# Writing the last third of a hybrid mixer in strict engine order, with its adaLN products placed one at a time

## The chip, the core and the metric

The kernel runs on one NeuronCore of a Trainium2 chip. The core has five engines, each with an instruction queue of its own: TensorE (PE; its weight loads are listed apart as PEld), VectorE (DVE), ScalarE (ACT), GpSimd (POOL) and SyncE (SP), which here issues nearly all DMA transfers. The metric is device time in microseconds (us) of one execution, lower is better; given is the median of several runs. A profiled execution has a span, from its first to its last instruction, and a time of its own.

## The reference

One decoder layer on 256 tokens (T) with 1024 channels (D), in float32. Nine vectors of 1024 come from `c @ w_ada + b_ada`: a shift, a scale and a gate for each of three parts.

```
h = rmsnorm(x, ffn1_norm) * (1 + sc1) + sh1
x = x + 0.5 * (1 + g1) * ((silu(h @ wg1) * (h @ wu1)) @ wd1)          # FFN 1, width 2816 = 22 * 128
h = rmsnorm(x, mix_norm) * (1 + sc2) + sh2
q_a, k_a, v_a, x_m, z = split(h @ w_in)                                # 5 times 512 columns
o_a = rmsnorm(attention(q_a, k_a, v_a), attn_norm)                     # 8 heads, causal
x_c = silu(causal_conv4(x_m))
h_m = groupnorm(mlstm(x_c, x_m)) * mlstm_norm                          # 4 heads
o_m = (h_m + mlstm_skip * x_c) * silu(z)
x = x + (1 + g2) * (concat(o_a, o_m) @ w_out)
h = rmsnorm(x, ffn2_norm) * (1 + sc3) + sh3
x = x + 0.5 * (1 + g3) * ((silu(h @ wg3) * (h @ wu3)) @ wd3)           # FFN 2
out = rmsnorm(x, final_norm)
```

With 256 tokens and blocks of 256, MoBA attention is plain causal attention. The mLSTM is computed for all 256 tokens at once instead of chunk by chunk.

## The kernel before

Everything is held transposed: channels on the 128 partitions, tokens along the free dimension, so x is 8 tiles of 128x256. Each product of a weight tile (128x128) with a tile of activations is done in three matmuls (`mm3`): weight and activation are each split in a high part in float32r and a low rest, and the matmuls are high x high, low x high, high x low.

**Weights.** They arrive as a fixed list of chunks of up to 128x2048 (1 MB), on the SP queue, into 4 buffers (`raw`). `weights()` takes the next chunk n: it issues the load of chunk n+3 and the split of chunk n+1, and returns chunk n. A split is done in pieces of 1024 columns: ScalarE copies the piece to float32r (`whi`), VectorE subtracts to get the rest (`wlo`). There are 5 buffers of each, so a piece can be split once the piece five before it has been used.

**adaLN products.** A vector element is 1024 products summed, so 128 of them are one VectorE instruction on a 128x1024 tile of w_ada (`ada`, 512 KB, 3 buffers), which writes 128 sums (output `junk` is not used). There are 72 of these. 16 (shift 1, scale 1) are written out at the start of FFN 1 and the last 8 (gate 3) belong to FFN 2; the 48 between stand in a list (`jobs`), and `side(0, 0)` takes the next two: their loads on SP and their products on VectorE. In order: gate 1, scale 2, shift 2, gate 2, scale 3, shift 3, eight each; behind the last of eight a small instruction or two finish the vector (`scale_fin`: tiles `fin`, `gs`; `shift_fin`: `sh`).

**Order.** A scheduler orders each engine's instructions at compile time, by its own estimate of the times. An engine wrapped in `Ordered` with `on` set pins each instruction behind the one written directly before it on the same engine (`keep_in_program_order`); instructions without a pin move wherever their data and buffers let them. DMA issues are always pinned. Inside the mixer the `ada` products are pinned too (`pinned`), each behind the VectorE instruction written just before it.

**The mixer's last third** stands at the end of `mixer`: value tile 1 (`values(1)`, generator `g0`), attention heads (`scores`, `turn` for the transposed probabilities, `weigh` for the product with the values, all by pairs of heads j), mLSTM heads (`m_scores`, `m_sums`, `m_vars`), then `a_out` (norm of the attention output: `rstd_of`, `oa`, split into `mix0` and `mix3`), four tiles of z (`tiles(shifted(zs...))`, each 24 `mm3` products' worth of matmuls in a "b" bank of PSUM, of which there are 2; `done` empties it with a `col` copy and a bias on ScalarE and a product `ht` on VectorE), `m_factors` (the norm factors of the mLSTM heads, a chain between ScalarE and VectorE on 4x256 tiles, which ends in `rows`), `z_silu`, and the product with w_out over four chunks c of two input tiles k each. Tiles k = 0 to 3 are `mix0` and `mix3`; k = 4, 5 come from `m_out(0)` and 6, 7 from `m_out(1)`, which multiply `cn` by the factors that `m_spread` puts in PSUM behind k = 1, add, multiply by silu(z) and split (`hh`, `hl`). Last, `residual` adds each output tile to x and forms the next FFN's input (`pre_h`: `hh`, `hl`) and its squares.

Before the change, TensorE, ScalarE and VectorE are pinned from `weigh(3)` to the first `next(g)` behind `a_out`, ScalarE and VectorE again in `m_factors` to `z_silu` and in the two `m_out`, and TensorE stays pinned up to c = 1. The splits of w_out and w_z, `m_sums(3)`, `m_skip`, the emptying of the z tiles and the residual are not.

Of the kernel before, what the change touches and what calls it, by code (L numbers as in the profile page):

```python
# [14 lines left out]
ALU = mybir.AluOpType  # L15
# [3 lines left out]
T = 256  # L19
# [42 lines left out]
def layer(ctx: ExitStack, tc: tile.TileContext, i, out: bass.AP):  # L62
    nc = tc.nc
    act, dve, pool, pe = (Ordered(tc, e) for e in (nc.scalar, nc.vector, nc.gpsimd, nc.tensor))
# [40 lines left out]
    x_sb = const([P, ND, T], F32, "x")  # L105
# [138 lines left out]
    gt = [const([P, ND], F32, f"gt{k}") for k in range(3)]  # L244
# [113 lines left out]
            eng.tensor_tensor(acc, acc, s, ALU.add)  # L358
        return s

    def residual(d, ps, g, k):
        dve.scalar_tensor_tensor(x_sb[:, d], ps, g[:, d:d + 1], x_sb[:, d], ALU.mult, ALU.add)
        if k is None:
            s = add_sq(d, pool)
            pool.tensor_scalar(fin_u[0][:, d], x_sb[:, d], sm[:, C_NF + d:C_NF + d + 1], None, ALU.mult)
            return s
        if k == 1:

            s = add_sq(d, pool)
            for j in range(2 * d - 6, 2 * d - 4) if 3 <= d < 6 else range(d, d + 1) if d >= 6 else ():  # L370
                pre_h(k, j)
        elif d == ND - 1:
            s = add_sq(d, pool)
            pre_h(k, d)
        else:
            pre_h(k, d)
            s = add_sq(d, pool)
        return s
# [26 lines left out]
    def ffn(k, nxt):  # L405
        nfa = 3
        with tc.tile_pool(name=f"g{k}", bufs=1) as gp:
            g2 = gp.tile([P, NF, 2, T], F32R, name=f"g2{k}")
            gh, gl = g2[:, :, 0], g2[:, :, 1]
            if k == 0:  # L410
# [34 lines left out]
                def keep(ft):  # L445
                    if ft % 2:
                        act.activation(half[:, ft], ps[ft], AF.Copy)
                    else:
                        dve.tensor_copy(half[:, ft], ps[ft])

                ps = [bank(t) for t in ring]
                r1 = rstd_of([sq[:, d] for d in (0, 1, 4, 5)], pre=False,
                             mid=lambda: (warm(16), ada(8), ada(0), load_to(0), scale_fin(0, 0, 1, pool),
                                         shift_fin(0, 0, 1, pool)))
# [21 lines left out]
                ps = [bank(t) for t in ring]  # L476
# [5 lines left out]
                        inner(w, f2, ps[2 * j + f2], 0, False)  # L482
                for d in range(4, 8):
                    w = weights()
                    side(1)
                    outer(w, ps, d, d == 7)

                late = [lambda ft=ft: finish(gh, gl, 8 + ft, ps[ft][:, 0:T], ps[ft][:, T:2 * T])
# [1 line left out]
                for j in range(4):  # L490
                    if j < 2:
                        late.pop(0)()
                        late.pop(0)()
                    w = weights()
                    if j == 3:
                        side(1)
                    for f2 in range(2):
                        ft = 2 * j + f2
                        pb = bank("a")
                        inner(w, f2, pb, 4, True)  # L500
                        o = half[:, ft]
                        dve.tensor_tensor(o, o, pb, ALU.add)
                        finish(gh, gl, ft, o[:, 0:T], o[:, T:2 * T])
                nfa = 16
            else:
                ps = [bank(t) for t in ("b", "b", "a", "a", "a", "a")]
# [56 lines left out]
    nxt_sq = [None]  # L563
# [3 lines left out]
    def side(*on):  # L567

        for o in on:
            if jobs:  # L570
                jobs.pop(0)(o)
# [9 lines left out]
    for c in range(2):  # L581
        w = weights()
        side(*[0] * (3 - 3 * c))
        for d4 in range(4):
            d = c * 4 + d4
# [10 lines left out]
    with tc.tile_pool(name="fin", bufs=1) as fp:  # L596
# [4 lines left out]
        r2 = r.unsqueeze(1).to_broadcast([P, 2, T])  # L601
# [5 lines left out]
def mixer(tc, nc, i, mp, L):  # L607
    act, dve, pool, pe, sp = L["act"], L["dve"], L["pool"], L["pe"], L["sp"]
# [3 lines left out]
    residual, newton, rstd_of, tables = L["residual"], L["newton"], L["rstd_of"], L["tables"]  # L612
    ident, ident_b, maskq, maskt, ohc, ohr = (L[k] for k in ("ident", "ident_b", "maskq", "maskt", "ohc", "ohr"))
    nxt_sq, r, px, acc2 = L["nxt_sq"], L["r"], L["px"], L["acc"]
    side, jobs = L["side"], L["jobs"]
# [1 line left out]
    def mt(shape, name, dt=F32, tag=None, bufs=1):  # L617
        return mp.tile(shape, dt, name=nm(name), tag=tag or name, bufs=bufs)

    def tiles(*done):  # L620

        w = weights()
        for g in range(2):
            pb = bank("b")
            for d in range(8):
                mm3(pb[:, 0:W], w, (g * 8 + d) * P, hh[:, d], hl[:, d], start=(d == 0), stop=(d == 7))
            done[g](pb)
            yield

    def shifted(dst):  # L630

        def done(pb):
            col = tmp.tile([P, 1], F32, tag="col", name=nm("col"), bufs=3)
            act.activation(col, pb[:, T:T + 1], AF.Copy)
            t = t256("ht", bufs=3)
            dve.tensor_tensor(t, r, pb[:, 0:T], ALU.mult)
            act.activation(dst, t, AF.Identity, bias=col)
        return done

    ones_h = mt([P, P], "ones_h")  # L640
# [83 lines left out]
    st = {}  # L724
# [68 lines left out]
    def m_sums(h):  # L793
        if h == 0:
            st["prow"] = bank("a")
        prow = st["prow"]
        pn = bank("b" if h == 3 else "m")
        pe.matmul(pn[:, 0:T], vm[:, 0, h], wE[h][:, 0:T], start=True, stop=False, skip_group_check=True)
        pe.matmul(pn[:, P:T], vm[:, 1, h], wE[h][:, T:384], start=False, stop=True, skip_group_check=True)
        pe.matmul(prow[0:4, 0:T], ohc[:, h], wE[h][:, 0:T], start=(h == 0), stop=False, skip_group_check=True)  # L800
        pe.matmul(prow[0:4, P:T], ohc[:, h], wE[h][:, T:384], start=False, stop=(h == NH - 1),
                  skip_group_check=True)
        act.activation(cn[:, h], pn[:, 0:T], AF.Copy, scale=sm[:, C_MN + h:C_MN + h + 1])
        s = st["sq", h] = t256("sq", bufs=3)
        act.activation(s, pn[:, 0:T], AF.Square)

    def m_vars(h):
        pe.matmul(st["prow"][0:4, T:2 * T], ohc[:, h], st["sq", h], start=False, stop=(h == NH - 1),
                  skip_group_check=True)

    def m_factors():


        prow, em = st["prow"], st["em"]
        act.on = dve.on = True
        dd = mt([NH, T], "dd", tag="R2")
        act.activation(dd, prow[0:4, 0:T], AF.Square, scale=EPS ** 0.5)
        dve.tensor_tensor(dd, dd, em, ALU.max)
        vv = mt([NH, T], "vv", tag="R3")
        dve.scalar_tensor_tensor(vv, prow[0:4, T:2 * T], 1.0 / P, dd, ALU.mult, ALU.add)  # L820
        rs = mt([NH, T], "rs", tag="R1")
        act.activation(rs, vv, AF.Ln)
        act.activation(rs, rs, AF.Exp, scale=-0.5)
        newton(rs, vv, [NH, T], "r", 0.0)
        spread(rs)
# [7 lines left out]
    zs = mt([P, NH, T], "zs")  # L833
# [15 lines left out]
    def m_out(h2):  # L849

        h = slice(2 * h2, 2 * h2 + 2)
        c = cn[:, h]
        dve.tensor_tensor(c, c, st["pb"][h2].rearrange("p (h t) -> p h t", t=T), ALU.mult)
        dve.tensor_tensor(c, c, xc[:, h], ALU.add)
        dve.tensor_tensor(c, c, zs[:, h], ALU.mult)
        k = slice(4 + 2 * h2, 6 + 2 * h2)
        hilo(hh[:, k, 0:T], hl[:, k, 0:T], c)
# [50 lines left out]
    def turn(j):  # L908

        for e in range(2):  # L910
            pt = bank("a")
            for b in range(3):
                pe.transpose(pt[:, b * P:(b + 1) * P], st["pr", j][:, e, b * P:(b + 1) * P], ident)
            pT = st["pT", j, e] = mt([P, 384], "pT", tag=f"pT{e}", bufs=2)
            act.activation(pT, pt[:, 0:384], AF.Copy)
# [15 lines left out]
            pool.tensor_tensor(acc2, acc2, s, ALU.add)  # L931

    def a_out():
        r2 = rstd_of([acc2, st["osq"]], ones_h, "a", pre=False)
        for j in range(4):
            o = oa[:, j, 0:T]
            dve.scalar_tensor_tensor(o, o, sm[:, C_AN + j:C_AN + j + 1], r2, ALU.mult, ALU.mult)

        mix3[:] = [mt([P, 3, T], name, F32R, tag="pr", bufs=2) for name in ("mix3h", "mix3l")]
        hilo(*mix0, oa[:, 0, 0:T])  # L940
        hilo(*mix3, oa[:, 1:4, 0:T])
# [3 lines left out]
    g = queries(0)  # L945
# [6 lines left out]
    g = queries(1)  # L952
# [11 lines left out]
    g = queries(2)  # L964
# [8 lines left out]
    g = queries(3)  # L973
# [17 lines left out]
    turn(2)  # L991
    m_scores(3)
    m_sums(1)
    g = tiles(shifted(zs[:, 0]), shifted(zs[:, 1]))
    side(0, 0, 0, 0, 0, 0)
    next(g)
    next(g0)
    turn(3)
    weigh(2)
    for e in (pe, act, dve):  # L1000
        e.on = True
    weigh(3)
    m_sums(2)
    m_vars(0)
    a_out()
    next(g)
    act.on = dve.on = False
    m_sums(3)
    m_skip()
    m_vars(1)  # L1010
# [6 lines left out]
    next(g)  # L1017
    z_silu(0)
    z_silu(1)
    act.on = dve.on = False  # L1020
    po = [bank(t) for t in ("m", "m", "a", "a")]
    for c in range(4):
        w = weights()
        side(*[0] * (0, 1, 2, 3)[c])
        pe.on = c < 2
        for k2 in range(2):
            k = c * 2 + k2
            for d in range(8):
                mm3(po[d // 2][:, (d % 2) * T:(d % 2 + 1) * T], w, (k2 * 8 + d) * P, *mix(k),
                    start=(c == 0 and k2 == 0 and d % 2 == 0), stop=(c == 3 and k2 == 1))  # L1030
                if (k, d) == (1, 7):
                    m_spread()
                    act.on = dve.on = True
                    m_out(0)
                    m_out(1)
                    act.on = dve.on = False
    side(*[0] * len(jobs))
    act.on = dve.on = True
    L["pre_shift"](2)
    act.on = dve.on = False  # L1040
    for d in range(8):
        nxt_sq[0] = residual(d, po[d // 2][:, (d % 2) * T:(d % 2 + 1) * T], L["gt"][1], 2)


# [84 lines left out]
```

## Time and profile before

| | |
|---|---|
| time, median of 3 runs | 532.76 us (532.58 to 534.71) |
| the profiled execution: time | 531.47 us |
| the profiled execution: span | 529.7 us |
| granted TensorE clock, mean | 0.995 |
| busy: PE, DVE, ACT, POOL | 97%, 80%, 53%, 9% |

The span is some 1.8 us shorter than the execution's own time. A profile line names an operation by its output and inputs (`wlo<-raw,whi`), with partitions x elements; as a helper records every operation, all have the same line number, and tile names tell them apart. A matmul's end is modelled and consecutive matmuls overlap in the listing; the distance between the starts of two neighbours is what one costs.

### The profile page before, as it was taken

Reading aid. Unit: us, or ns where it says so; the run is one execution under the profiler, and the core shown is the slowest. Engines: PE = TensorE matmul, PEld = TensorE weight load, DVE = VectorE, ACT = ScalarE, POOL = GpSimd, SP = SyncE. Lnnn points to the kernel's source line nnn. Section 1 sums busy time; section 2 is a strip of 40 time slices with the busy share of each in tenths; the row PEclk is TensorE's granted clock in tenths of the full one; section 3 lists DMA queues with packets and bytes.
Section 4 is the critical chain, followed back from the end, with each engine's and each line's share of the span. In section 5 each row is a group of like instructions: output and inputs, shape, how many; then the busy total and the mean of one; then the engine's idle time right before and its main releaser. Section 6 shows DMA issues by size and latency. Waiting matters only on the chain.

```text
span 529.7 us, 9595 instructions
## 1 busy us (share of the span) xinstructions
PE 511.9 (97%) x3826; PEld 480.0 (91%) x3826; DVE 422.3 (80%) x703; ACT 282.9 (53%) x484; POOL 45.5 (9%) x60
## 2 busy tenths in 40 slices
PE   8999999999999999999999988999999999999992
PEld 7889999999988889988877888999999999988891
DVE  7799977998889997997869887989887777655423
ACT  4364436655645444569766554865555545544410
POOL 5000000000001110120000001300000000022220
PEclk9999999999999999999999999999999999999997
DMA  8999985677878887783115963578764554464002
GB/s 306 363 368 379 376 357 201 251 278 287 321 294 298 335 329 290 282 354 120 41 41 198 400 227 103 206 301 307 285 241 160 171 215 171 161 220 178 0 1 79
DMA packets 24095, 125.73 MB, mean 237 GB/s; under 512 B 2673, under 2 KB 3185, under 8 KB 14578
## 3 DMA queue, kind: packets, MB, share of 16 engines
q1 hardware_dynamic: 23762, 124.72, 62.4%
q8 instruction: 30, 0.49, 0.4%
q10 hardware_dynamic: 288, 0.39, 0.2%
q14 instruction: 15, 0.12, 0.1%
HBM read 124.05 MB, written 1.05 MB: 236 GB/s over the span
## 4 chain that ended last, share of the span: by engine, by line
PE 87%; DVE 6%; DMA 3%; ACT 2%; issue 1%; SPq 0%; DVEq 0%; ACTq 0%
PE psa L55 44%; PE psb L55 24%; PE psm L55 19%; DVE junk L55 2%; DMA ada<-in_ada 2%; DVE wlo L55 1%; ACT whi L55 1%; DMA x<-in_x 1%; DVE u_out L55 0%; DVE ht L55 0%; ACT sq L55 0%; DVE oa L55 0%; DVE hl L55 0%; DVE nw L55 0%; ACT hh L55 0%
## 5 line engine op out<-in xcount | busy, mean ns | idle before, releaser
L55 ACT ACTIVATE whi<-raw 128x1024 fp32r<-128x1024 f32 (+1 forms) x160 | 166.8, 1047 | 128.1 <-PE psa L55 78.7
L55 DVE TENSOR_TENSOR wlo<-raw,whi 128x1024 fp32r<-128x1024 f32 (+1 forms) x160 | 193.7, 1214 | 45.0 <-ACT whi L55 43.5
L55 PE MATMUL psa<-hh,wlo 128*128 128x256 f32 (+1 forms) x440 | 123.3, 281 | 0.0
L55 PE MATMUL psa<-hh,whi 128*128 128x256 f32 (+1 forms) x440 | 123.1, 282 | 0.0
L55 PE MATMUL psa<-hl,whi 128*128 128x256 f32 (+1 forms) x440 | 122.1, 280 | 0.0
L55 DVE SCALAR_TENSOR_TENSOR junk<-ada,c_bc 128x1024 bf16<-128x1024 f32 x72 | 89.8, 1248 | 11.8 <-DMA ada<-in_ada 11.5
L55 PEld LDWEIGHTS psa<-hh,wlo 128*128 128x128 f32 x440 | 83.1, 189 | 0.1
L55 PEld LDWEIGHTS psa<-hh,whi 128*128 128x128 f32 x440 | 82.9, 189 | 0.0
L55 PE MATMUL psb<-hh,whi 128*128 128x258 f32 (+1 forms) x284 | 82.1, 290 | 0.8 <-ACT whi L55 0.6
L55 PEld LDWEIGHTS psa<-hl,whi 128*128 128x128 f32 x440 | 82.7, 189 | 0.0
L55 PE MATMUL psb<-hh,wlo 128*128 128x258 f32 (+1 forms) x284 | 80.5, 284 | 0.4 <-DVE wlo L55 0.4
L55 PE MATMUL psb<-hl,whi 128*128 128x258 f32 (+1 forms) x284 | 79.6, 282 | 0.0
L55 PE MATMUL psa<-g,whi 128*128 128x512 f32 (+1 forms) x198 | 59.8, 369 | 0.0
L55 PEld LDWEIGHTS psb<-hh,whi 128*128 128x128 f32 x284 | 53.7, 189 | 3.0 <-ACT whi L55 1.0
L55 PEld LDWEIGHTS psb<-hh,wlo 128*128 128x128 f32 x284 | 53.8, 189 | 1.7 <-issue 1.0
L55 PEld LDWEIGHTS psb<-hl,whi 128*128 128x128 f32 x284 | 53.5, 190 | 0.0
L55 PE MATMUL psa<-g,wlo 128*128 128x256 f32 x176 | 45.9, 281 | 0.0
L55 PE MATMUL psm<-hh,whi 128*128 128x256 f32 (+1 forms) x156 | 43.9, 282 | 1.7 <-ACT hh L55 1.7
L55 PE MATMUL psm<-hl,whi 128*128 128x256 f32 (+1 forms) x156 | 43.7, 282 | 0.5 <-DVE hl L55 0.4
L55 PE MATMUL psm<-hh,wlo 128*128 128x256 f32 (+1 forms) x156 | 43.8, 281 | 0.0
L55 PEld LDWEIGHTS psa<-g,whi 128*128 128x128 f32 x198 | 35.2, 188 | 6.2
L55 PEld LDWEIGHTS psa<-g,wlo 128*128 128x128 f32 x176 | 32.1, 188 | 0.6
(251 smaller groups left out, 777.5 us busy)
## 6 DMA issues: line engine op xcount, KB each, us to landing
ada<-in_ada SPq DMA_DIRECT2D x72, 512.0 KB, 5.9
raw<-in_dn SPq DMA_DIRECT2D x22, 1024.0 KB, 4.8
raw<-in_guB SPq DMA_DIRECT2D x19, 1024.0 KB, 4.8
raw<-in_gu SPq DMA_DIRECT2D x18, 1024.0 KB, 7.3
raw<-in_gu SPq DMA_DIRECT2D x8, 512.0 KB, 7.4
raw<-in_wqk SPq DMA_DIRECT2D x4, 1024.0 KB, 6.3
raw<-in_wout SPq DMA_DIRECT2D x4, 1024.0 KB, 7.7
raw<-in_guA SPq DMA_DIRECT2D x4, 768.0 KB, 4.6
```

Of the source, the lines that this page charges most:

```text
L55: r = f(*a, **k)
```

## The change

FFN 1 takes three more `ada` products, so every later `side` call takes the product three places further down the list. In the mixer the six products in front of the first z tile become one; others stand singly behind `weigh(2)`, behind `m_sums(2)`, in `a_out` between the reciprocal root and its Newton steps, and one in front of each of the chunks c = 0, 1, 2. From the first z tile to the residual, TensorE, ScalarE and VectorE are pinned throughout, except ScalarE's copies for the split made at c = 1. `tiles` can hand back between a tile's matmuls and its emptying. `m_out(1)` moves behind the split at c = 1. The residual's add of tile d comes ahead of the norm instructions of tile d - 1.

```
-    def residual(d, ps, g, k):
-        dve.scalar_tensor_tensor(x_sb[:, d], ps, g[:, d:d + 1], x_sb[:, d], ALU.mult, ALU.add)
+    def residual(d, ps, g, k, add=True):
+        if add:
+            dve.scalar_tensor_tensor(x_sb[:, d], ps, g[:, d:d + 1], x_sb[:, d], ALU.mult, ALU.add)
...
                 for d in range(4, 8):
                     w = weights()
-                    side(1)
+                    side(*[1] * (1 + d // 7))
                     outer(w, ps, d, d == 7)
...
                     w = weights()
-                    if j == 3:
+                    if j != 1:
                         side(1)
...
-    def tiles(*done):
+    def tiles(*done, apart=False):
...
+            if apart:
+                yield
             done[g](pb)
             yield
...
         prow, em = st["prow"], st["em"]
-        act.on = dve.on = True
...
-        r2 = rstd_of([acc2, st["osq"]], ones_h, "a", pre=False)
+        r2 = rstd_of([acc2, st["osq"]], ones_h, "a", pre=False, mid=lambda: side(0))
...
     turn(2)
     m_scores(3)
     m_sums(1)
-    g = tiles(shifted(zs[:, 0]), shifted(zs[:, 1]))
-    side(0, 0, 0, 0, 0, 0)
+    for e in (pe, act, dve):
+        e.on = True
+    g = tiles(shifted(zs[:, 0]), shifted(zs[:, 1]), apart=True)
+    side(0)
     next(g)
     next(g0)
+    next(g)
     turn(3)
     weigh(2)
-    for e in (pe, act, dve):
-        e.on = True
+    side(0)
     weigh(3)
     m_sums(2)
+    side(0)
     m_vars(0)
     a_out()
     next(g)
-    act.on = dve.on = False
+    next(g)
     m_sums(3)
     m_skip()
     m_vars(1)
...
     z_silu(0)
     z_silu(1)
-    act.on = dve.on = False
     po = [bank(t) for t in ("m", "m", "a", "a")]
     for c in range(4):
+        act.on = c != 1
         w = weights()
-        side(*[0] * (0, 1, 2, 3)[c])
-        pe.on = c < 2
+        act.on = True
+        if c == 1:
+            m_out(1)
+        side(0)
         for k2 in range(2):
...
                 if (k, d) == (1, 7):
                     m_spread()
-                    act.on = dve.on = True
                     m_out(0)
-                    m_out(1)
-                    act.on = dve.on = False
     side(*[0] * len(jobs))
-    act.on = dve.on = True
     L["pre_shift"](2)
-    act.on = dve.on = False
-    for d in range(8):
-        nxt_sq[0] = residual(d, po[d // 2][:, (d % 2) * T:(d % 2 + 1) * T], L["gt"][1], 2)
+    x_sb, gt = L["x_sb"], L["gt"]
+    for d in range(9):
+        if d < 8:
+            dve.scalar_tensor_tensor(x_sb[:, d], po[d // 2][:, (d % 2) * T:(d % 2 + 1) * T], gt[1][:, d:d + 1],
+                                     x_sb[:, d], ALU.mult, ALU.add)
+        if d:
+            nxt_sq[0] = residual(d - 1, None, None, 2, False)
+    act.on = dve.on = pe.on = False
```

## Rows read from the trace of the kernel before

**Rows 1.** The page, busy time of each engine, share of the span, instructions.

```profile
PE 511.9 (97%) x3826; PEld 480.0 (91%) x3826; DVE 422.3 (80%) x703; ACT 282.9 (53%) x484; POOL 45.5 (9%) x60
```

**Rows 2.** Windows, mixer's end: stretch, its length, busy by engine, clock, DMA share, GB/s.

```profile
280.00:300.00 20.00, 19.22 (x141) 15.85 (x140) 18.79 (x34) 11.53 (x27) 1.14 (x1) 1.00 0.83 312
300.00:320.00 20.00, 18.39 (x149) 17.72 (x148) 16.79 (x26) 10.95 (x17) 0.00 (x0) 1.00 0.65 240
320.00:340.00 20.00, 18.21 (x147) 17.69 (x146) 16.89 (x31) 14.41 (x29) 6.16 (x7) 1.00 0.33 113
```

**Rows 3.** Timeline of TensorE: start, duration, operation, and in brackets idle and releaser.

```profile
284.62 1.63 PE L55 MATMUL psa<-pT,va 128*64 128x256 f32 x16 [0.60 <-ACT va L55]
...
288.98 0.47 PE L55 MATMUL psb<-hh,whi 128*128 128x258 f32 x1
...
294.40 0.39 PE L55 MATMUL psb<-hh,whi 128*128 128x258 f32 x1
...
301.23 0.28 PE L55 MATMUL psm<-mix0h,whi 128*128 128x256 f32 x1
...
308.36 0.92 PE L55 MATMUL psb<-rows,ohr 36*128 36x256 f32 x4 [1.24 <-DVE rows L55]
...
323.15 0.39 PE L55 MATMUL psm<-hh,whi 128*128 128x256 f32 x1 [1.67 <-ACT hh L55]
...
329.26 0.28 PE L55 MATMUL psb<-hh,whi 128*128 128x258 f32 x1
```

**Rows 4.** The chain that ended last: start, duration, what; twelve matmuls of w_out.

```profile
302.82 1.45 PE psa L55 x12
```

**Rows 5.** Timeline of VectorE, 279 to 310 us.

```profile
279.88 1.22 DVE L55 SCALAR_TENSOR_TENSOR junk<-ada,c_bc 128x1024 bf16<-128x1024 f32 x1
...
281.02 1.22 DVE L55 TENSOR_TENSOR wlo<-raw,whi 128x1024 fp32r<-128x1024 f32 x1
...
287.17 0.57 DVE L55 TENSOR_TENSOR fin<-mod,b 128x8 f32<-128x8 f32 x1
...
293.85 1.68 DVE L55 SCALAR_TENSOR_TENSOR oa<-oa,sm,rr 128x256 f32<-128x256 f32 x4
...
296.92 0.95 DVE L55 TENSOR_TENSOR mix3l<-oa,mix3h 128x768 fp32r<-128x768 f32 x1
...
306.54 1.22 DVE L55 SCALAR_TENSOR_TENSOR junk<-ada,c_bc 128x1024 bf16<-128x1024 f32 x1
...
307.79 0.41 DVE L55 TENSOR_TENSOR rows<-rs,rows 4x256 fp32r<-4x256 f32 x1
...
309.71 0.68 DVE L55 TENSOR_TENSOR cn<-cn,psb 128x512 f32<-128x512 f32 x1
```

**Rows 6.** Timeline of ScalarE, 270 to 312 us.

```profile
270.91 0.53 ACT L55 ACTIVATE xc<-xc,sm 128x256 f32<-128x256 f32 x1
...
284.45 0.87 ACT L55 ACTIVATE pT<-psa 128x384 f32<-128x384 f32 x2
...
295.61 0.83 ACT L55 ACTIVATE mix3h<-oa 128x768 fp32r<-128x768 f32 x1
...
301.43 1.06 ACT L55 ACTIVATE whi<-raw 128x1024 fp32r<-128x1024 f32 x1 [0.95 <-PE psb L55]
...
309.23 1.28 ACT L55 ACT_TABLE_LOAD   x1
310.52 1.16 ACT L55 ACTIVATE zs<-zs 128x512 f32<-128x512 f32 x2
```

**Rows 7.** Timeline of the SP queue, 225 to 350 us: the issues between two w_out loads.

```profile
243.96 43.53 SPq L98 DMA_DIRECT2D ada<-in_ada  x7
```

**Rows 8.** Windows, two stretches of FFN 1.

```profile
78.90:84.50 5.60, 5.60 (x52) 5.60 (x51) 3.70 (x6) 4.73 (x7) 0.00 (x0) 1.00 0.55 195
...
95.80:101.40 5.60, 5.60 (x50) 5.60 (x49) 5.60 (x10) 3.36 (x6) 0.00 (x0) 1.00 0.50 192
```

**Rows 9.** Windows, behind the last matmul.

```profile
524.00:530.00 6.00, 0.00 (x0) 0.00 (x0) 1.45 (x4) 0.00 (x0) 0.00 (x0) 0.50 0.57 175
```

## The prediction, written before the change was run

> **What bounds the kernel now.** I read the page's busy shares first. TensorE is listed busy for 97% of the span, VectorE for 80%, ScalarE for 53% [rows 1], so a step costs or gives time only where TensorE waits for it. The windows of the mixer's end come next: in the 60 us from 280 on, TensorE has no listed work for 0.78 + 1.61 + 1.79 = 4.2 us, while VectorE is busy for 16.8 to 18.8 of each 20 us [rows 2]. Nothing that the change does there can win much more than these 4.2 us. TensorE's timeline says where they lie: 0.60 us in front of `weigh(2)` (for `va`), 1.24 us in front of `m_spread` (for `rows`), 1.67 us in front of k = 6 (for `hh` of `m_out(1)`) [rows 3]. Third, the timelines of VectorE and ScalarE, which feed it. The product at 306.54 stands in front of `rows` at 307.79, though its chunk is written later [rows 5]: the scheduler's choice made that wait. But the same freedom lets ScalarE split a piece the moment a buffer is free: the copy at 301.43 waited for nothing but TensorE's last use of a buffer at 301.4, ahead of its place in the text [rows 6].
>
> **Loads.** The SP queue spends 43.5 us over seven `ada` loads while a w_out load stands behind them [rows 7]. The change puts one product in front of that load in place of six, so it starts some 20 us earlier. I count that at nothing: TensorE shows no wait for it.
>
> **FFN 1: three products more.** Each is 1.14 us of VectorE, the distance from the start of a product to the next instruction [rows 5], and a load of 0.5 MB. Two stretches give the cover: where the first is put VectorE is busy 3.70 of 5.60 us; where the third is put it is full, 5.60 of 5.60, and DMA has half its time free [rows 8]. The third makes a backlog of about 1.1 us. A split piece is used only after four others, four times 2.9 us (two rows like [rows 4]), so the backlog reaches no matmul. Price 0; with the cover gone it would be 1.1 us.
>
> **The written order, step by step.** Every queue now keeps the order of the text, so I walk the three queues with durations from the rows. The value tile and first z tile hold the same matmuls in either order; I leave TensorE's end of the first z tile where it is, near 282.8.
>
> *(a) `weigh(3)`.* VectorE's product at 279.88 is now followed by a second one, by both splits for the second z chunk (before, these lay earlier), and only then by `ht` of the first z tile: 279.88 + 4 x 1.14 + 0.4 = 284.9, or 285.5 if `scale_fin` (0.57) falls in between [rows 5]. ScalarE cannot pass: its `zs` (0.5) and the two `pT` (0.87) follow [rows 6], so the first `pT` is there at 285.8 to 286.4. Before, `weigh(3)` began in the middle of the 16 matmuls from 284.62, at 285.4 [rows 3]. What stands behind it, up to the second z tile at 288.98, moves by +0.4 to +1.0, and where the end of the scale comes first other small waits join it: I take +0.9 from the range 0 to +1.3.
>
> *(b) third z tile.* It needs a "b" bank, which `ht` of the second empties. That `ht` now stands behind all of `a_out`: from the norm's sum 0.9 (two activations of 0.4 and 0.5), Newton 3 x 0.45, `oa` 1.6, `mix3h` 0.83, `mix3l` 0.87, `ht` 0.42 and hand-overs, 6.2 us [rows 5, 6]. TensorE meanwhile has 294.40 - 288.98 = 5.4 us of work [rows 3]. A wait of +0.8, less some 0.3 that the old order lost in front of the fourth tile. So w_out begins at 301.23 [rows 3] + 0.9 + 0.5 = 302.6.
>
> *(c) behind k = 1.* From that `ht` on ScalarE writes `zs`, `cn`, a square (1.1), four `xc` at 0.4, the two copies for w_out chunk 0 (2.0); VectorE's second split and the next `ht` end 6.3 us behind the first. `zs` 0.5; the factor chain, nine steps of some 0.4 to 0.45 [rows 5], to 10.9; `col`, `ht`, `zs` of the last tile to 11.8; table load 1.28, two silu 1.16 [rows 6], to 14.2; and only then the copy for chunk 1, 1.06, to 15.3, and its low part, 1.22, to 16.5. TensorE has 3.0 + 0.5 + 3.0 for the two tiles, four times 1.43 for k = 0 and 1 [rows 4], 0.92 for `m_spread` [rows 3]: 13.1. It waits 2.2 us for the first matmul of chunk 1 and 1.2 more for the second: 3.4. The old wait at this place was 1.24, for `rows`, which now are early.
>
> The Trainium skill (ScalarE: Activation LUTs, What ACT_TABLE_LOAD costs) gives a drain of about 1.38 us besides the load's 1.28. The trace has the load's 1.28 and the silu right behind it, 0.01 us later [rows 6]; with that drain the sum would be 1.4 us more, by the trace it is as above.
>
> *(d) k = 4 and k = 6.* From here VectorE sets the pace. Between the first split piece of chunk 1 and that of chunk 2 it has a split 1.14, a product 1.14, `m_out(0)` with 3 x 0.7, ScalarE's copy 0.6 and the low part 0.7, a split 1.2: 6.9 us; TensorE has 5.7 for a chunk [rows 4, 5]. Wait 1.2. To chunk 3 the count is the same, with `m_out(1)` and the next product: 1.2. Before: 1.67 at k = 6 and some 0.4 at k = 4, so these two places are about even.
>
> *(e) FFN 2.* VectorE then has a split, the last product and `sh`, the splits of 1024 and 512, two small `hl`, x of tiles 0 and 1 and `hl` of tile 0, 6.0 us, against 5.7. Wait 0.3. Alternating add and norm brings the first tile early and the last x some 5 us later, which frees two of FFN 2's six banks; the other four give TensorE 12 matmuls, 1.4 us, for each of the first tiles, so nothing waits. Price 0; without that cover up to 1 us.
>
> **Sum.** 302.6 + 5.7 + 0.9 + 3.4 + 5.7 + 1.2 + 5.7 + 1.2 + 5.7 + 0.3 = 332.4, against 329.26 for FFN 2's first matmul [rows 3]: +3.1 us. Behind that the two kernels are the same. The profiled execution took 531.47 (span 529.7), so 534.6; it lies 1.3 below the median of the runs, 532.76, to which the prediction goes: 535.9.
>
> **Rivals.** *The order keeps ahead (faster).* Three products fewer are 3.4 us of VectorE in a stretch where it is nearly full. If the splits of chunk 1 end before k = 1 does, all waits go, up to 4.2 us: 528.6 to 530.0. It decides at the copy for chunk 1: it would have to be done 3.4 us earlier than I count. Against it: the text puts it behind silu. Chance 0.16.
>
> *Even.* The chain enters the last two z tiles with no lateness. Then only the factor chain (5.5 us for `zs` and factors against 3.5 for a tile) is late, the wait behind k = 1 falls to about 1.3, and the sum to 0 to +1.5: 532.8 to 534.3. For it: loads and splits in front of the stretch can lie differently. Chance 0.20.
>
> *The clock.* Granted is 1.00 all through, waits of 1.67 us included; behind the last matmul a stretch without any reads 0.50 [rows 2, 3, 9]. A wait of 3.4 us in the middle, longer than any here, might let it fall: one chunk at 1.2 GHz instead of 2.4 costs 5.7 us more, 541.6. Chance 0.05. The Trainium skill (TensorE: Matmul & The Clock Gate, Why this matters for your kernels) warns that idle gaps between bursts of matmuls bring the half rate back; no row here shows it inside the kernel.
>
> *FFN 1 pays* its 1.1 us on top: 537.0. Chance 0.04.
>
> **The numbers.** The forecast has 0.55, with its own range 534.3 to 537.4 (the +0 to +1.3 of (a), 0.8 either way in (c)). Half a per cent, 2.7 us, is about what a measurement of this kernel tells from no change (the three runs span 2.1). Of the forecast's 0.55, 0.36 lie over it. Slower: 0.36 + 0.05 + 0.04 = 0.45; same: 0.19 + 0.20 = 0.39; faster: 0.16. The range 530.0 to 537.9 leaves out the faster case but for its upper edge, and the clock: under 2 in 10.
>
> **What would show it.** In the profile after: a TensorE wait in front of k = 2 with `whi` and then `wlo` as releasers, 3 us or more in all; under 1.5 would make (c) wrong. No wait for `rows`. The third z tile's matmuls behind `ht`, with an idle of about 0.8. In VectorE's timeline a gap of some 3 to 4 us between `ht` of the last z tile and the first split of chunk 1. FFN 1 unchanged, with w_in beginning within 0.3 us of where it did. The prediction is wrong if FFN 2 begins at 330 or earlier.

## The result, and the profile after the change

The changed kernel takes 536.31 us, the median of nine runs; eight lie from 536.04 to 538.33, the ninth, disturbed, took 2,844.88. The kernel before, run nine times beside it, takes 533.71 (531.09 to 536.77). The ratio is 1.0056, 95% interval 1.0034 to 1.0078: slower, by little more than what can be told from no change. The prediction was 535.9, 1.0059 times the median that it started from.

The profiled execution took 538.33 us (span 536.5), against 531.47 before. Each kernel was later profiled once more: 536.09 (span 534.3) and 531.98 (span 530.2). The page of the first profile after, busy time and share of the span:

```profile
PE 516.7 (96%) x3826; PEld 484.8 (90%) x3826; DVE 421.2 (78%) x703; ACT 283.2 (53%) x484; POOL 47.0 (9%) x60
```

TensorE is listed 4.8 us longer than before for the same 3826 matmuls [rows 1], which a slower clock would do. The windows of the same profile, with the columns of [rows 2], and two shorter stretches:

```profile
280.00:300.00 20.00, 18.24 (x129) 14.43 (x128) 12.95 (x25) 12.47 (x28) 0.83 (x1) 1.00 0.50 193
300.00:320.00 20.00, 16.70 (x115) 16.07 (x114) 12.79 (x20) 10.06 (x17) 0.00 (x0) 0.83 0.38 131
320.00:340.00 20.00, 18.24 (x139) 17.83 (x138) 18.99 (x33) 12.34 (x24) 4.40 (x6) 0.91 0.51 186
311.54:318.36 6.82, 5.96 (x26) 5.66 (x27) 5.89 (x8) 3.60 (x5) 0.00 (x0) 0.50 0.46 138
335.43:338.84 3.41, 3.27 (x15) 3.27 (x16) 3.41 (x9) 2.77 (x7) 2.46 (x4) 0.50 0.60 250
```

TensorE without listed work has grown from 4.2 to 1.76 + 3.30 + 1.76 = 6.8 us. VectorE has fallen from 18.79 and 16.79 to 12.95 and 12.79 us in the first two windows and has 18.99 in the third, where it had 16.89: part of its work now comes later. The granted clock is at its lower level, 1.2 GHz (0.50), in two stretches where the kernel before keeps 2.4 GHz (1.00). TensorE's timeline (start, duration, operation, idle and releaser):

```profile
289.31 0.47 PE L55 MATMUL psb<-hh,whi 128*128 128x258 f32 x1
...
295.97 0.39 PE L55 MATMUL psb<-hh,whi 128*128 128x258 f32 x1 [1.17 <-DVE ht L55]
...
302.56 0.28 PE L55 MATMUL psm<-mix0h,whi 128*128 128x256 f32 x1
...
308.37 0.73 PE L55 MATMUL psb<-rows,ohr 36*128 36x256 f32 x4
311.72 0.58 PE L55 MATMUL psm<-mix3h,whi 128*128 128x256 f32 x1 [2.62 <-ACT whi L55]
312.98 0.58 PE L55 MATMUL psm<-mix3h,wlo 128*128 128x256 f32 x1 [0.68 <-DVE wlo L55]
...
315.07 0.41 PE L55 MATMUL psm<-mix3h,wlo 128*128 128x256 f32 x1
315.28 0.41 PE L55 MATMUL psm<-mix3l,whi 128*128 128x256 f32 x1
...
334.18 0.39 PE L55 MATMUL psb<-hh,whi 128*128 128x258 f32 x1 [1.60 <-ACT hh L55]
...
335.57 0.80 PE L55 MATMUL psb<-hl,whi 128*128 128x258 f32 x2 [0.17 <-DVE hl L55]
```

The old wait for `rows` at `m_spread` is gone [rows 3]. In its place stands one behind k = 1, first for the high part of chunk 1 (2.62), then for its low part (0.68 listed; the starts are 1.26 apart where 0.12 is usual). Chunk 1 then runs at 0.21 us a matmul (315.07 to 315.28). At FFN 2's door, its first matmul, there is a new wait of 1.60. VectorE, and below it ScalarE, in the timelines of the same profile:

```profile
280.73 2.36 DVE L55 TENSOR_TENSOR wlo<-raw,whi 128x1024 fp32r<-128x1024 f32 x2 [0.62 <-ACT whi L55]
283.94 0.42 DVE L55 TENSOR_TENSOR ht<-rr,psb 128x256 f32<-128x256 f32 x1 [0.85 <-ACT col L55]
...
295.50 0.41 DVE L55 TENSOR_TENSOR ht<-rr,psb 128x256 f32<-128x256 f32 x1
...
307.30 0.42 DVE L55 TENSOR_TENSOR ht<-rr,psb 128x256 f32<-128x256 f32 x1
311.70 2.36 DVE L55 TENSOR_TENSOR wlo<-raw,whi 128x1024 fp32r<-128x1024 f32 x2 [3.98 <-ACT whi L55]
...
329.04 2.96 DVE L55 TENSOR_TENSOR wlo<-raw,whi 128x1024 fp32r<-128x1024 f32 x3
...
332.07 0.87 DVE L55 SCALAR_TENSOR_TENSOR x<-psm,gt,x 128x256 f32<-128x256 f32 x2
332.86 0.69 DVE L55 TENSOR_TENSOR wlo<-raw,whi 128x512 fp32r<-128x512 f32 x1
333.75 1.23 DVE L55 TENSOR_TENSOR wlo<-raw,whi 128x1024 fp32r<-128x1024 f32 x1 [0.21 <-ACT whi L55]
334.90 0.62 DVE L55 SCALAR_TENSOR_TENSOR hl<-x,gs,hh 128x256 fp32r<-128x256 f32 x1
```

```profile
306.40 0.42 ACT L55 ACTIVATE rows<-rs 4x256 fp32r<-4x256 f32 x1 [1.37 <-DVE rs L55]
...
308.28 1.28 ACT L55 ACT_TABLE_LOAD   x1
309.57 1.15 ACT L55 ACTIVATE zs<-zs 128x512 f32<-128x512 f32 x2
310.63 3.88 ACT L55 ACTIVATE whi<-raw 128x1024 fp32r<-128x1024 f32 x4
...
332.67 1.06 ACT L55 ACTIVATE whi<-raw 128x1024 fp32r<-128x1024 f32 x1 [2.18 <-PE psa L55]
333.63 0.49 ACT L55 ACTIVATE hh<-x,gs 128x256 fp32r<-128x256 f32 x1
```

Two places are to be seen. ScalarE copies chunk 1 at 310.63, behind the table load and both silu; before, such a copy had been done at 301.43 [rows 6]. And at FFN 2's door, pieces of FFN 2's second and third chunks come before `hh` and `hl` of tile 0, for which TensorE waits: on VectorE one low part ahead of the first two x (the last of the three at 329.04; the other two are the first chunk's) and two behind them (332.86, 333.75), on ScalarE a copy at 332.67. These splits are written by FFN 2's first two `weights()`, behind the last pin, so nothing holds them to their place in the text.

The time goes by stretches as follows (starts in TensorE's timelines, as us behind the first matmul of w_in):

| | before | before, again | after | after, again |
|---|---|---|---|---|
| w_in begins at | 202.38 | 202.21 | 202.88 | 202.24 |
| second z tile | 86.59 | 86.59 | 86.43 | 86.42 |
| third z tile | 92.01 | 92.02 | 93.08 | 93.08 |
| w_out, k = 0 | 98.85 | 99.44 | 99.67 | 99.66 |
| `m_spread` | 105.97 | 106.57 | 105.49 | 105.47 |
| k = 2 | 106.83 | 107.42 | 108.84 | 108.83 |
| k = 4 | 112.62 | 113.21 | 118.16 | 117.79 |
| FFN 2 | 126.88 | 127.54 | 131.29 | 131.13 |
| last matmul | 317.68 | 318.33 | 324.05 | 322.45 |

FFN 2 begins 3.6 to 4.4 us later. Behind that the first profile after loses 2.0 us more than before, the second 0.5. The first also has w_in 0.5 us late. The moved products are not the reason: a matmul that starts at 33.17 before and at 33.21 in the second profile after starts at 33.66 in the first, ahead of all of them; in its first 14 us the granted clock is 0.88, where the second has 1.00.

### The profile page after: what moved, and what is told of

Same layout as the page of the kernel before. It is cut to its first block, busy times and chain, and to the rows that moved or that the text cites. A ratio compares the mean times of both kernels' runs of the same rounds, so it can differ in the third digit from the quotient of the medians.

```text
span 536.5 us, 9595 instructions
## 1 busy us (share of the span) xinstructions
PE 516.7 (96%) x3826; PEld 484.8 (90%) x3826; DVE 421.2 (78%) x703; ACT 283.2 (53%) x484; POOL 47.0 (9%) x60
## 4 chain that ended last, share of the span: by engine, by line
PE 92%; DVE 3%; ACT 3%; DMA 1%; issue 0%; DVEq 0%; SPq 0%; ACTq 0%
PE psa L55 46%; PE psb L55 25%; PE psm L55 21%; DVE wlo L55 1%; DMA x<-in_x 1%; ACT whi L55 1%; ACT zs L55 1%; DVE sq L55 0%; DVE u_out L55 0%; DVE nw L55 0%; DVE ht L55 0%; ACT xc L55 0%; ACT L55 0%; ACT rs L55 0%; ACT mix3h L55 0%
```

## The experiments

The kernel before ran beside each group on the same chip: 533.40 (32 runs) with the first four, 533.42 (29 runs) with the next four, 532.32 (7 runs) with the last. Ratios are to these.

**Chunk 1's split ahead of silu.** On the changed kernel:

```
     next(g)
+    L["split_to"](L["used"][0] + 1)
     z_silu(0)
```

> The changed kernel with one step moved: the split of w_out chunk 1 (both copies and both low parts) is written in front of the two silu instead of behind them, pinned as before. Theory (the copy is late because it stands behind the table load and silu): TensorE's wait in front of k = 2 falls from 2.62 + 0.68 us to about 1.3 in all, the clock stays at 1.00 there, and the time falls by 2.5 to 3.5 us against the changed kernel, to 533 to 534. Rival (VectorE's total work paces the stretch, wherever the copy stands): the wait only moves to k = 4 and k = 6, gain under 1 us.

Measured 534.23 (533.76 to 535.47), ratio 1.0004 (0.9978 to 1.0029), 2.1 us under the changed kernel, where 2.5 to 3.5 were expected. TensorE's timeline:

```profile
308.76 0.38 PE L55 MATMUL psm<-mix3h,whi 128*128 128x256 f32 x1 [0.16 <-ACT whi L55]
310.01 0.39 PE L55 MATMUL psm<-mix3h,wlo 128*128 128x256 f32 x1 [0.88 <-DVE wlo L55]
...
316.94 0.38 PE L55 MATMUL psm<-hh,wlo 128*128 128x256 f32 x1 [0.96 <-DVE wlo L55]
...
323.80 0.38 PE L55 MATMUL psm<-hh,wlo 128*128 128x256 f32 x1 [0.89 <-DVE wlo L55]
...
331.13 0.39 PE L55 MATMUL psb<-hh,whi 128*128 128x258 f32 x1 [1.59 <-ACT hh L55]
```

The wait for `whi` is gone and the chunk runs at the higher clock. Now waits for VectorE come out at k = 4 and k = 6, 0.96 and 0.89, which the profile after, with its late and slow chunk 1, does not show. So the copy's place behind silu is a cause, and VectorE's pace behind it is another.

**Holding the clock.** On the changed kernel, 22 products of a 128x128 tile of ones behind `m_spread`, so that TensorE does not stand still; they are no part of the computation.

```
                 m_spread()
+                fill = bank("a")
+                for _ in range(22):
+                    pe.matmul(fill[:, 0:P], ones_h, ones_h, start=True, stop=True)
                 m_out(0)
```

> The changed kernel with 22 extra matmuls of 128x128 without use behind the spread of the factors, some 2.5 us of work, where TensorE waits for chunk 1. If the low clock costs what its slower matmuls cost: chunk 1 is done 2.4 us sooner and the kernel is about 2 us faster. If VectorE paces the stretch: the clock stays at 1.00, but waits of about 1.2 us come up in front of k = 4 and k = 6, and the time is within 0.7 us of the changed kernel.

Measured 536.22 (535.80 to 537.77), ratio 1.0048 (1.0020 to 1.0075): the changed kernel's time. A window in chunk 1 of this run:

```profile
311.50:315.50 4.00, 4.00 (x37) 4.00 (x36) 3.96 (x6) 2.14 (x3) 0.00 (x0) 1.00 0.32 69
```

and its only wait in w_out behind the filling, in front of k = 6 (TensorE's timeline):

```profile
325.83 0.38 PE L55 MATMUL psm<-hh,wlo 128*128 128x256 f32 x1 [0.89 <-DVE wlo L55]
```

The clock is held at 2.4 GHz. The filling took 5.2 us, so k = 2 begins 111.07 us behind w_in, 2.2 later than before the filling; k = 4 comes at 116.84, 1.0 to 1.3 earlier, and FFN 2 at 131.14, the same: what was won at k = 4 is lost again in the wait for VectorE at k = 6. VectorE, busy 3.96 of 4.00 us in the window, sets FFN 2's start whichever clock chunk 1 has. The low clock there cost nothing in the end.

**The three products alone.** On the kernel before, the three products more in FFN 1 and no new pins. The order that the scheduler may choose so is the free order below; that of the changed kernel is the strict order.

```
-                    side(1)
+                    side(*[1] * (1 + d // 7))
...
-                    if j == 3:
+                    if j != 1:
                         side(1)
```

> The kernel before with only the three products more in FFN 1, so that the list is used up three places earlier in the mixer. Theory (FFN 1 hides them): w_in begins within 0.3 us of where it did, and the chunks of w_out, freed of three products on VectorE, lose 0 to 1.5 us: same or slightly faster than before. Rival (VectorE is full in FFN 1): up to 1.1 us later at w_in, slower by up to 1 us.

Measured 531.61 (529.59 to 534.61), ratio 0.9951 (0.9921 to 0.9981): faster by half a per cent. w_in begins at 202.42, as in the kernel before. In its profile the wait at k = 6 is gone, the one for `rows` stands as before, one for `ht` in front of the fourth z tile is 1.25 (0.18 and 0.77 in the two profiles of before), and the clock falls behind them:

```profile
299.39 0.39 PE L55 MATMUL psb<-hh,whi 128*128 128x258 f32 x1 [1.25 <-DVE ht L55]
...
309.49 0.93 PE L55 MATMUL psb<-rows,ohr 36*128 36x256 f32 x4 [1.24 <-DVE rows L55]
```

```profile
310.73:314.14 3.41, 3.41 (x19) 3.41 (x18) 2.27 (x4) 2.07 (x3) 0.00 (x0) 0.50 0.15 57
```

FFN 1 hides the products, and what they free is worth some 1.8 us by the medians. The loss of the whole change is thus in what it does to the order.

**The old residual.** On the changed kernel the residual of before, unpinned:

```
-    for d in range(9):
-        if d < 8:
-            dve.scalar_tensor_tensor(x_sb[:, d], po[d // 2][:, (d % 2) * T:(d % 2 + 1) * T], gt[1][:, d:d + 1],
-                                     x_sb[:, d], ALU.mult, ALU.add)
-        if d:
-            nxt_sq[0] = residual(d - 1, None, None, 2, False)
     act.on = dve.on = pe.on = False
+    for d in range(8):
+        nxt_sq[0] = residual(d, po[d // 2][:, (d % 2) * T:(d % 2 + 1) * T], L["gt"][1], 2)
```

> The changed kernel with the residual as before the change: unpinned, add and norm of one tile together. Theory (FFN 2's first copy and low parts, unpinned, slip in between the pinned add and norm of tile 0): FFN 2's first wait falls from 1.60 us to under 0.5, gain 1 to 1.5 us against the changed kernel. Rival (the wait is due to VectorE being late from the chunks, whatever the order of the residual): the wait stays over 1 us and the time is within 0.5 us.

Measured 539.53 (538.40 to 540.00), ratio 1.0093 (1.0063 to 1.0123): worse than the changed kernel, where a gain was expected. TensorE's and VectorE's timelines at the door:

```profile
333.58 0.39 PE L55 MATMUL psb<-hh,whi 128*128 128x258 f32 x1 [1.59 <-ACT hh L55]
...
337.51 0.51 PE L55 MATMUL psb<-hl,whi 128*128 128x258 f32 x2 [1.49 <-DVE hl L55]
```

```profile
333.81 1.65 DVE L55 SCALAR_TENSOR_TENSOR x<-psa,gt,x 128x256 f32<-128x256 f32 x4
335.37 1.21 DVE L55 TENSOR_TENSOR wlo<-raw,whi 128x1024 fp32r<-128x1024 f32 x1
336.51 2.71 DVE L55 SCALAR_TENSOR_TENSOR hl<-x,gs,hh 128x256 fp32r<-128x256 f32 x3
```

The door's wait of 1.59 stays, so the pinned alternation of add and norm is not its cause. Without it four adds go first, then a split, and `hl` comes only from 336.51, which adds a wait of 1.49: pinning add and norm in turn is the good part of the change.

**FFN 2's second split behind four tiles.** On the changed kernel, in the residual's loop:

```
             nxt_sq[0] = residual(d - 1, None, None, 2, False)
+        if d == 4:
+            L["split_to"](L["used"][0] + 1)
```

> The changed kernel with one thing written down that it left to the scheduler: the split of FFN 2's second chunk stands, pinned, behind the norm of tile 3 in the residual. Theory (that split slips in front of the norm of tile 0): FFN 2's first wait falls from 1.60 us to under 0.5, the two small ones behind it go, the clock stays at 1.00 there, and the time falls by 2 to 3 us, to about 534. Rival (VectorE is simply late from w_out): the wait stays over 1 us, or comes up again in front of FFN 2's tile 2, gain under 0.7 us.

Measured 535.11 (534.94 to 536.28), ratio 1.0038 (1.0015 to 1.0060): 1.2 us under the changed kernel, where 2 to 3 were expected. The first matmul of FFN 2 no longer waits, and begins 129.38 us behind w_in, 1.8 to 1.9 earlier. ScalarE's timeline of this run has the splits behind the fourth tile:

```profile
333.05 0.51 ACT L55 ACTIVATE hh<-x,gs 128x256 fp32r<-128x256 f32 x1
...
333.77 2.51 ACT L55 ACTIVATE whi<-raw 128x1024 fp32r<-128x1024 f32 x3
```

Two smaller waits come later, 0.24 and 0.52 for these splits. The third chunk's first piece is held behind the second chunk's, and comes late with it. The cause of the door's wait is the place of these splits.

**Both edits.** The first and the fifth experiment's lines together.

> The changed kernel with both repairs: chunk 1's split in front of the silu, and FFN 2's second split written into the residual. If the two losses are apart, the gains add: 2.1 us measured for the first and some 2 for the second, to 532, with waits of about 1.1 us left in front of k = 2, 4 and 6. If both are one backlog of VectorE, the sum stays at the larger of the two, 534.

Measured 532.77 (532.34 to 533.21), ratio 0.9988 (0.9969 to 1.0007): the gains add, 2.1 and 1.2 against 3.5. Placing two splits gives the loss back.

**Six products in FFN 1, free order.** On the kernel before, six more instead of three:

```
-                    side(1)
+                    side(*[1] * (1 + (d in (4, 7))))
...
-                    if j == 3:
-                        side(1)
+                    side(1)
...
-                if k or ft > 16:
+                if k or ft > 15:
```

> The kernel before with six products more in FFN 1 in place of three. Theory (FFN 1 hides what its backlog allows): w_in begins within 0.3 us of where it did, time 0 to 1 us under that of three products, 530.5 to 531.6. Rival (VectorE is full there and the fourth to sixth reach a matmul): w_in begins 1 to 3 us later, slower than with three.

Measured 527.47 (527.06 to 527.85), ratio 0.9884 (0.9851 to 0.9917): the fastest of all, 3 us under what was expected. Windows of this run:

```profile
280.00:300.00 20.00, 19.40 (x143) 16.10 (x142) 17.48 (x30) 11.88 (x28) 1.13 (x1) 1.00 0.71 277
300.00:320.00 20.00, 19.90 (x164) 19.44 (x163) 14.46 (x23) 11.69 (x19) 0.00 (x0) 1.00 0.39 127
320.00:340.00 20.00, 20.00 (x166) 19.90 (x165) 17.28 (x28) 15.26 (x28) 7.17 (x7) 1.00 0.54 198
```

TensorE is without listed work for 0.7 us where it was 4.2 [rows 2], and w_in begins at 202.23. VectorE is busy for 1.3 and 2.3 us less in the first two windows and 0.4 more in the third. The products' loads moved with them; no run parts what each of the two is worth.

**Six products, strict order.** The changed kernel with the two lines of the sixth experiment and the three further products.

> Both repairs and six products more in FFN 1 than the kernel before, so that none is left in the chunks of w_out. If VectorE's pace of 6.9 us per chunk made the waits in front of k = 4 and k = 6, it is now 5.75 and both fall under 0.3 us: 2 us faster than with both repairs alone, about 530. If something else made them, no gain.

Measured 531.37 (530.83 to 531.90), ratio 0.9962 (0.9941 to 0.9984): 1.4 us under the sixth experiment, where 2 were expected. At equal products in FFN 1 the strict order, as the change writes it and with both splits put right, costs 3.9 us against the free order. The windows of this run:

```profile
280.00:300.00 20.00, 18.23 (x129) 14.44 (x128) 12.98 (x25) 12.47 (x28) 0.82 (x1) 1.00 0.47 173
300.00:320.00 20.00, 18.48 (x150) 17.75 (x149) 14.45 (x21) 10.02 (x17) 0.00 (x0) 1.00 0.27 89
320.00:340.00 20.00, 19.40 (x162) 18.99 (x161) 15.40 (x27) 13.38 (x27) 6.11 (x7) 1.00 0.49 176
```

TensorE lacks 1.77 + 1.52 + 0.60 = 3.9 us, 3.2 more than with free order, though VectorE is busy for 6.4 us less: it is not the amount of VectorE's work there but its order that TensorE waits for. The clock is 1.00 in these windows of both, so the clock is no part of this difference.

**Second profiles.** Both kernels as they are.

> The kernel before, unchanged, profiled once more. The runs of the kernel before spread from 530.8 to 537.4 us while those of the changed one lie at 536.0 to 538.3. Theory: the spread of the kernel before comes from stretches at a granted clock of 0.50 that some of its executions have behind a wait in w_out and others do not, each worth a part of 3.4 us; then this execution shows one, at about 533 to 536 us, or none, at about 531. Rival: it comes from the transfers in front of w_in; then w_in begins at another time than 202.4 us and what lies behind it takes the same as before.

> The changed kernel, unchanged, profiled once more. Theory: the waits come from the written order, so the first matmul of chunk 1 waits again 2.6 us for its high part and the one behind it for the low part, FFN 2's door waits again some 1.7 us, and the distance from the start of w_in to FFN 2's first matmul is 131 us within 0.5. What may differ is the number of stretches at a granted clock of 0.50: the runs at 536 have one fewer than the first profiled execution at 538.3.

531.98 and 536.09. The kernel before has no stretch at 0.50 up to its last matmul, and nothing in front of w_in moved, so this profile shows no cause of its spread. The mean granted clock listed for each run speaks for the first theory: of the 68 runs of the kernel before that ran beside the experiments, the 21 at 0.994 or 0.995 took 530.79 to 532.96 us, the 17 at 0.989 or less 533.04 to 537.35. Both profiled executions are of the first kind, so no trace shows where the others lose the clock. The changed kernel repeats its waits (2.63, 0.68, 1.59) and its distance to FFN 2 (131.13). Behind the door its clock stays up:

```profile
334.00:338.00 4.00, 3.83 (x32) 3.62 (x32) 4.00 (x10) 3.05 (x9) 2.97 (x5) 1.00 0.78 309
```

From FFN 2's start to the last matmul it takes 191.32 us, the first profile 192.76: the stretch at 1.2 GHz behind the door, the one difference of clock between the two behind w_in, was worth 1.4 us.

**Eight products in FFN 1, free order.** On the seventh experiment `side(1, 1)` for each d from 4 to 7. (The bound in the seventh's last line also goes down to 14, without effect, as `ft` starts at 16.)

> The kernel before with eight products more in FFN 1 (six gave 527.47), nothing else. Theory that FFN 1 still has room: w_in begins at 202.2 us within 0.3 and the two products fewer behind it give little or nothing more, since only waits of 0.77 and 0.26 us were left: 526.5 to 527.5. Rival, FFN 1 is full: VectorE's backlog reaches a matmul, w_in begins 1 us or more later, and the time is 528 to 530.

Measured 527.72 (527.50 to 528.00), ratio 0.9914 (0.9880 to 0.9948). w_in begins at 202.17, so FFN 1 still hides them, but nothing more is gained; the second z tile comes 0.5 us later.

**Order alone.** The kernel before, products where they stood, with the three engines pinned from the first z tile to the end of the residual (ScalarE's copies at c = 1 excepted).

```
     m_sums(1)
+    for e in (pe, act, dve):
+        e.on = True
     g = tiles(shifted(zs[:, 0]), shifted(zs[:, 1]))
     side(0, 0, 0, 0, 0, 0)
```

> The kernel before with the three engines pinned in written order from the first z tile to the residual (ScalarE's copies at c = 1 excepted), and every product where it stood: six in front of the first z tile, one, two and three in front of c = 1, 2, 3. Theory that strict order by itself costs some 4 us at equal products, and that setting the products singly was needed under it: 540 us or more, with a wait of 4 to 7 us in front of the first z tile or the weighing behind it, where six products of 1.14 stand on VectorE. Rival, the order itself is harmless and the loss of the changed kernel is in the places it gave the splits: 533 to 537.

Measured 548.48 (547.72 to 548.90), ratio 1.0301 (1.0270 to 1.0331). TensorE's timeline:

```profile
292.13 2.88 PE L55 MATMUL psa<-pT,va 128*64 128x256 f32 x16 [8.99 <-ACT va L55]
```

VectorE runs the six products one behind another, waiting for their loads as well, to 288.4, and everything for the value tile stands behind them. The second z tile begins 96.0 us behind w_in, 9.6 later than in the changed kernel; that is most of the 12.2 us between the two. Setting the products singly is, by this wait, what makes the strict order bearable.

## Why the prediction came out

**Right in its main mechanism; in its sum partly by luck.** The slower case held 0.45, and the forecast's main step, (c), is there almost to the number: 3.4 us expected behind k = 1, and from `m_spread`'s start to the second matmul of chunk 1 TensorE takes 312.98 - 308.37 = 4.6 us where 0.9 and 0.12 are work, so 3.6. The order of the releasers, the absent wait for `rows`, the idle 3.98 of VectorE in front of the split and the start of w_in within 0.3 us (202.24 in the second profile) came as said (in the first profile w_in is 0.5 late). The first experiment shows the cause by removing it: 2.62 falls to 0.16, and 0.88 for the low part is left. The last has the same wait with the order alone (2.61 and 0.68), so the products are not its cause.

**(a) was mis-sized.** Expected +0.9, measured -0.2 for the second z tile. The walk let VectorE's queue start at 279.88 with a second product behind it. In fact what stands in front was early too: the scaling of the last attention probabilities began at 275.86 where it had been 278.96, and both splits began at 280.73, ending near 283.1 where the walk had 284.4. The written order did this, not FFN 1's products. VectorE's timelines of the third experiment, which has those products and the free order, and of the last, which has the strict order alone, begin this scaling at:

```profile
279.02 1.00 DVE L55 TENSOR_SCALAR pr<-pr,ri 128x128 f32<-128x128 f32 x4
...
275.13 1.01 DVE L55 TENSOR_SCALAR pr<-pr,ri 128x128 f32<-128x128 f32 x4
```

In the free order two of the splits of z weights stand at 263.27 and 268.80, between the steps of attention; pinned, they stand behind the scaling. The walk put them there, but did not credit the work in front with the 2.4 us that they leave.

**(b)** The third z tile waits 1.17 for `ht` (0.8 expected), and w_out begins 0.2 to 0.8 us later relative to w_in, by which profile of before is taken, where (a) and (b) together had 1.4. Removed by no experiment: that the `ht` behind `a_out` makes this wait is read from the releaser alone, and it stands in every kernel with the strict order.

**(d)** The waits at k = 4 and k = 6 do not show in the profile after, but they were not wrong: with chunk 1 on time they come, 0.96 and 0.89 against 1.2 each.

**(e) was mis-sized most.** The door's wait is 1.60 + 0.17, not 0.3. The walk counted the splits that stand pinned in front of the residual, and missed that the next ones are not pinned and slip in front of the adds and between them and tile 0's norm; the fifth experiment shows it. The price of the residual's order was put at nothing, up to 1; the fourth shows that in this place the old order costs some 3 us more, so the new one is a gain.

**The sum** came within 0.4 us because two errors cancel. Its waits make 3.4 + 1.2 + 1.2 + 0.3 = 6.1 against 1.24 + 0.4 + 1.67 = 3.3 before, +2.8, and with the 1.4 of (a) and (b) +4.2, yet it said +3.1: the walk took 5.7 us for a chunk where the stretch of before leaves (28.03 - 3.3 - 0.92) / 4 = 5.95 [rows 3]. Measured is +3.6 to +4.4. What was then added, 1.3 us from the profiled execution to the median, fits the kernel before, whose two profiled executions, 531.47 and 531.98, lie in the lower quarter of its 77 runs (530.79 to 537.35), but not the changed kernel, whose second, 536.09, lies 0.2 under its median. So +4.1 between the profiles of 531.98 and 536.09 is +2.6 between the medians: a sum 1.0 short met an allowance 1.1 too large. The clocks of the other runs of the kernel before point to stretches at 0.50 that its two profiles do not have; where these lie stays open.

**The rivals.** The clock does fall in the wait, which had 0.05: 0.50 from 311.54 on. The Trainium skill (TensorE: Matmul & The Clock Gate, Why this matters for your kernels) warns of half rate after idle gaps; this trace agrees, with 0.50 from the end of the idle 2.62 us on. But its price was not the 5.7 us of that rival: chunk 1 took 9.32 us instead of 5.79, 1.1 of it the wait for the low part, and the second experiment shows that none of it reached FFN 2's start, for which VectorE was the later one. Only the stretch behind the door cost, 1.4 us, in one profile of two. FFN 1 paid nothing, with three, six and eight products (w_in at 202.42, 202.23 and 202.17 in free order). The faster case needed chunk 1's copy 3.4 us earlier; the first experiment has it 2.5 us earlier behind w_in and comes to no change, since VectorE's pace takes over at k = 4 and k = 6. That speaks against this rival's "all waits go"; the full 3.4 us were not run. The Trainium skill (ScalarE: Activation LUTs, What ACT_TABLE_LOAD costs) has a drain of about 1.38 us besides the load; this trace does not show it: as before the change, the silu follows 0.01 us after the load's 1.28 (308.28 to 309.57).

**Where the gain went.** By the medians: three products moved to FFN 1 bring 533.4 to 531.6 (-1.8); strict order with the two splits put right costs 1.2 of it (532.8); the two splits' places cost 3.5 more (536.3). With six products in FFN 1 strict order costs 3.9. The 1.2 is too small a price for the order by itself: ten of the twelve runs with three products and free order have a mean clock of 0.990 or less, and the two at 0.994 took 529.59 and 530.17, while the runs of the sixth experiment took 532.34 to 533.21 at 0.991 to 0.994.

## What to carry to other kernels

Take work off the engine that is nearly full where another stage has room, before touching the order: six products moved into FFN 1, with the scheduler left free, gave the largest gain of all runs, 1.2%. If an order is written out, each split has to stand where its buffer comes free, not where its chunk is next spoken of, and the first unpinned instruction behind the stretch belongs to the walk too. Sum a forecast from differences of waits, not from rebuilt positions, and take the profiled execution's place among all runs as a term with its own uncertainty.

## What the runs showed of the hardware

The granted clock fell to 0.50 inside several kernels, and the length of the wait in front does not tell when. The kernel before keeps 1.00 through a wait of 1.67 us in both its profiles [rows 2, 3]; the third experiment falls at 310.73 behind waits of 1.25 and 1.24. The first and the sixth have the same waits in front of chunk 1, 0.16 and 0.88: the first keeps 1.00 there, the sixth has 0.50 from 310.16 to 313.57. Of the changed kernel's two profiles, with the same door wait of 1.60 and 1.59, one falls there and one does not. In the last experiment, with its wait of 8.99 us, it reads 0.50 for 10.24 us:

```profile
285.64:295.88 10.24, 3.75 (x18) 2.69 (x19) 5.07 (x7) 3.29 (x8) 0.72 (x1) 0.50 0.91 354
```

Here a stretch at 0.50 cost only where TensorE set the pace: nothing in chunk 1 of the changed kernel, 1.4 us at its door.
